# A two-block F32 network on one core: state-space preparation moved into the first feed-forward block, gate rows through DRAM, another SBUF layout

## The chip, the cores and the metric

The kernel runs on one core of a Trainium2 chip. The metric is the time of one execution on the device, in microseconds. In the profile, PE is TensorE's matmul stream, PEld its weight loads, DVE is VectorE, ACT ScalarE, POOL GpSimd, and SP is SyncE, which here only issues transfers.

## The reference

Two blocks run one after the other on 512 tokens of width 1024, both of depth 2. The first block is an attention block, which the change touches through the SBUF layout alone. The second has, in each layer, a feed-forward block, a token mixer and a second feed-forward block, each ahead of a gated residual sum:

```python
for l in range(DEPTH):
    mod = (silu(c) @ mod_w[l] + mod_b[l]).reshape(bsz, N_SUB, 3, D_MODEL)
    def pre(x, i):          return rms_norm(x, norm_pre[l, i]) * (1 + mod[:, i, 1]) + mod[:, i, 0]
    def post_add(x, y, i, w): return x + w * mod[:, i, 2] * rms_norm(y, norm_post[l, i])
    x = post_add(x, swiglu(pre(x, 0), ffn_w_in[l, 0], ffn_w_out[l, 0]), 0, 0.5)
    x = post_add(x, token_mixer(pre(x, 1), ...), 1, 1.0)
    x = post_add(x, swiglu(pre(x, 2), ffn_w_in[l, 1], ffn_w_out[l, 1]), 2, 0.5)

def s5_ssm(u, a_re, a_im, log_dt, b_re, b_im, c_re, c_im, d_skip):   # inside the mixer
    lam_bar = exp(lam * dt)                     # weights alone
    b_bar = ((lam_bar - 1) / lam)[..., None] * b  # weights alone
    states = scan(lam_bar, einsum(u, b_bar))    # over the 512 tokens
    return real(einsum(c, states)) + d_skip * u
```

The state-space part has 32 groups of 16 channels with 64 complex states each. All that depends on `a`, `log_dt`, `b` and `c` alone can be worked out before `u` is known.

## The kernel before

**Products.** All large products are F32 products made of three passes with F32R operands: each operand is held as a high and a low part, and `mm3` issues high×high, high×low and low×high (L336 to L338). The weights come through `unit`: SP loads 512 KB into a `raw` tile (3 slots, L316), ACT casts the high part into `wh` (3 slots, L319) and DVE subtracts to get the low part `wl` (3 slots, L320). Activations, and everything of 4 KB per partition, live in a pool called `big` with 34 slots. In `mm3` the weights are the stationary operand and 512 tokens move; in `tokens` (L413 to L415) the activations are stationary and the weights move, of which some are in `wh` and `wl` and the others, kept, in `big` tiles.

**Where tiles lie.** The pools get their SBUF addresses in the order in which the first tile of each tag is asked for. The built program has the tags `raw`, `wh`, `wl`, `tmp`, `hf` and `ms` at addresses that leave 32 on division by 64 bytes, since a tile `hpi` of 4 bytes is allocated ahead of them; `big` and `ones` leave 0.

**The feed-forward block** (`ffn`) goes in three parts p of 8, 7 and 7 column blocks. Each part first makes its `mid` tiles in a `glu` loop, two products (48 matmuls) per block, and then, in `tokens`, four passes over the 128-token groups that add `mid @ w_out` into `y`. POOL takes the low part of every second block (L428), DVE the others. While these run, `mod_job` streams the modulation weights of a layer through `ms` tiles and reduces them on DVE (L1001); for both layers this is over by the end of layer 0. Between p = 0 and p = 1, `gate_row` spreads a row of `mod` over the partitions by 8 F32 matmuls against the identity (L461) and two ACT copies, and `ssm_params` computes the small per-state numbers on DVE.

**The mixer** interleaves three generators by counters (`MIX`): attention, the gate products, and `ssm`. For each quarter q of 128 channels, `ssm` loads `ssmbc` (256 KB), forms the complex product `bl` with 6 DVE operations (`cplx`, L1221 to L1226), transposes it on PE (8 F32 transposes, L1246) into `gt`, forms `cl` and the rotations `cs` with 11 POOL operations on 128x512 (L1216, L1258, L1261 and `cplx`), forms the direct kernel `kt` on PE (L1276, L1279) and DVE; all of that depends on weights alone. Then come the parts that need the tokens: input products (L1290), the scan, the state `hh` on POOL and DVE (L1310 to L1315) and the output `y_ps`: per 128 columns j, j+1 direct products of 128x128 (L1322, F32) and 8 products with 32 output rows (L1325). The program's order on each engine is fixed when it is built.

Of the kernel before, what the change touches and what calls it, by code (L numbers as in the profile page):

```python
# [240 lines left out]
class Net:  # L241
    def __init__(self, ctx, tc, io, stop=None):
        self.tc, self.nc, self.io, self.stop = tc, tc.nc, io, stop
        nc = self.nc
        self.sb = ctx.enter_context(tc.tile_pool(name="sb", bufs=1))
        self.ps = ctx.enter_context(tc.tile_pool(name="ps", bufs=1, space=PSUM))
        self.dr = ctx.enter_context(tc.tile_pool(name="dr", bufs=1, space=DRAM))
        self.n, self.odd, self.turn, self.jobs, self.pace = 0, False, 0, [], None
        self.xd = io["x"]
        self.xf = [self.big() for _ in range(4)]  # L250
        self.ones = self.sb.tile([128, 128], F32, name="ones")
        nc.vector.memset(self.ones, 1.0)
        self.mhalf = self.sb.tile([128, 16], F32, name="mhalf")
        nc.vector.memset(self.mhalf, -0.5)
        self.hpi = self.sb.tile([128, 1], F32, name="hpi")
        nc.vector.memset(self.hpi, math.pi / 2)

    def constants(self):
        nc, io = self.nc, self.io
        cst = self.sb.tile([128, C_TAB], F32, name="cst")  # L260
        nc.sync.dma_start(cst, io["consts"][:, :C_TAB])
        self.cst = cst
        self.ident = cst[:, C_ID:C_ID + 128]
        self.mask = self.sb.tile([128, 3, 128], F32R, name="mask")
        for i, o in enumerate((C_ID, C_TRI, C_PERM)):
            nc.scalar.copy(self.mask[:, i], cst[:, o:o + 128])
        self.par = []
        for l in range(DEPTH):
            t = self.sb.tile([128, P_N], F32, name=f"par{l}")
            nc.sync.dma_start(t, io["params"][l])  # L270
            self.par.append(t)
# [704 lines left out]
    def mod_job(self, l):  # L976
# [29 lines left out]
        for i in range(3):  # L1006
            sc = mod[:, i * 24 + 8:i * 24 + 16]
            gt = mod[:, i * 24 + 16:i * 24 + 24]
            nc.vector.scalar_tensor_tensor(sc, in0=sc, scalar=1.0, in1=par[:, P_NPRE + 8 * i:P_NPRE + 8 * i + 8],
                                           op0=ALU.add, op1=ALU.mult)  # L1010
            nc.vector.tensor_scalar(sc, sc, 32.0, None, op0=ALU.mult)
            nc.vector.scalar_tensor_tensor(gt, in0=gt, scalar=32.0 if i == 1 else 16.0,
                                           in1=par[:, P_NPOST + 8 * i:P_NPOST + 8 * i + 8],
                                           op0=ALU.mult, op1=ALU.mult)


    def gate_row(self, l, i):

        o = self.big((128, D))
        k = i * 24 + 16  # L1020
        for m, a in enumerate(self.halves(o)):
            self.nc.scalar.copy(a, self.bcast(self.mod[l][:, k + 4 * m:k + 4 * m + 4]))
        return o
# [16 lines left out]
    def ffn(self, l, i, h, nxt, between):  # L1040
        nc = self.nc
        h = self.acts(h)
        y = [self.big((128, D)) for _ in range(4)]
        for p, n in enumerate(SPLIT_K):
            mid = self.pairs(n)
# [15 lines left out]
            for j, f in enumerate(fs):  # L1061
                if j < nh:
                    continue
                f(*[self.mblock(self.wk(f"in{i}"), h) for _ in range(2)], FULL)
                self.pace = mid[j][:, 0, 0:1].bitcast(F32)
                self.pump(2)
            acts = [(t[:, 0], t[:, 1]) for t in mid]
# [9 lines left out]
            if p == 0:  # L1077
                gate = self.gate_row(l, i)
                if i == 0:
                    self.ssm_p = self.ssm_params(l)  # L1080

        if callable(nxt):
            nxt = nxt()
# [118 lines left out]

    def ssm(self, l, P, u, ud, out):

        nc = self.nc
        v, g = nc.vector, nc.gpsimd
        d4 = [128, 4, 4, 32]

        def v4(t):
# [8 lines left out]
        def cplx(e, o, a, b, c, d, view):  # L1218
# [7 lines left out]
            e.tensor_tensor(o[:, 1], o[:, 1], t[:, 1], op=ALU.add)  # L1226

        for q in range(4):
            pq = slice(q * 4, q * 4 + 4)
# [5 lines left out]
                      for c in range(2))  # L1235
            f0, f1 = (f[:, pq].unsqueeze(3).to_broadcast(d4) for f in P["f"])
            cplx(v, bl, b0, b1, f0, f1, v4)
            bb = self.tmp(256)
            nc.scalar.copy(bb.rearrange("p (c a b) -> p c a b", c=2, a=4),
                           bl.rearrange("p c (a j b) -> p c a j b", a=4, j=4)[:, :, :, 3])  # L1240
            gt = self.big()
            for c in range(2):
                ps = self.t("aux", [128, 512])
                for i in range(4):
                    s = slice(i * 128, (i + 1) * 128)
                    nc.tensor.transpose(ps[:, s], bl[:, c, s], self.ident)  # L1246
                if c:
                    nc.scalar.copy(gt[:, c], ps)
                else:
                    v.tensor_copy(gt[:, c], ps)  # L1250
            nc.scalar.mul(bc[:, 3], bc[:, 3], -1.0)
# [14 lines left out]
            cplx(g, cs, *ta, *tb, lambda t: t.rearrange("p (a b c) -> p a b c", a=4, b=8))  # L1266
            ct, st = cs[:, 0], cs[:, 1]
            ru = self.big()
            rho = v3(ru[:, 0])
            nc.scalar.copy(rho, P["rho"][:, pq].unsqueeze(2).to_broadcast([128, 4, 128]))  # L1270
            g.memset(rho[:, :, 0:1], 0.0)
            nc.sync.dma_start(ru[:, 1], ud[q])
            yield 1
            ps = self.t("aux", [128, 512])
            for c in range(2):
                nc.tensor.matmul(ps[:, 0:128], lhsT=bb[:, c * 128:(c + 1) * 128], rhs=bc[:, 2 + c],  # L1276
                                 start=c == 0, stop=c == 1)
            for c in range(2):
# [4 lines left out]
            v.scalar_tensor_tensor(kt[:, 0], in0=self.ident, scalar=self.par[l][:, P_SD + q:P_SD + q + 1],  # L1283
                                   in1=kt[:, 0], op0=ALU.mult, op1=ALU.add)
            sp = []
            for c in range(2):
# [13 lines left out]
            g.tensor_tensor(zi, zi, t[:, 1], op=ALU.subtract)  # L1300
            v.tensor_tensor_scan(zr, ru[:, 0], zr, 0.0, op0=ALU.mult, op1=ALU.add)
            v.tensor_tensor_scan(zi, ru[:, 0], zi, 0.0, op0=ALU.mult, op1=ALU.add)
            yield 1
# [13 lines left out]
            y_ps = self.t("yps", [128, 512])  # L1317
            uq = u[q // 2][:, q % 2]
            for j in range(4):
                o = y_ps[:, j * 128:(j + 1) * 128]  # L1320
                for a in range(j + 1):
                    nc.tensor.matmul(o, lhsT=kt[:, j - a], rhs=uq[:, a * 128:(a + 1) * 128], start=a == 0, stop=False)  # L1322
                for c in range(2):
                    for i in range(4):
                        nc.tensor.matmul(o[i * 32:(i + 1) * 32], lhsT=cl[:, c, j * 128 + i * 32:j * 128 + i * 32 + 32],  # L1325
                                         rhs=hh[:, c, i * 128:(i + 1) * 128], start=False, stop=c == 1)
            t = self.big()
# [9 lines left out]
    def mixer(self, l, h, nxt, between):  # L1337
        nc, par = self.nc, self.par[l]
        P = self.ssm_p
        h = self.acts(h)  # L1340
# [44 lines left out]
        side.s = side.g = 0  # L1385
        S_ = self.ssm(l, P, u, ud, gl)
        G_ = gated()
        next(S_)
        n = 0
# [115 lines left out]
    def run(self):  # L1505
        nc = self.nc
        self.mod = [None] * DEPTH
        h1 = self.newh()

# [50 lines left out]
```

## Time and profile before

| | |
|---|---|
| time, median of 3 runs | 3297.89 us (3291.76 to 3299.95) |
| the profiled execution: time, span | 3300.94 us, 3299.2 us |
| mean granted TensorE clock | 0.991 |
| SP's transfers | 377.31 MB, 33.9% of the 16 engines' time |

The span runs from the first to the last instruction. The ends of matmuls are modelled, so a duration of a matmul in the profile is longer than the step to the next one; steps are read from starts. All transfers of the kernel before are issued by SP.

### The profile page before, as it was taken

The page shows a single profiled execution, that of the slowest core. Times are in us where ns is not written, and L with a number is a line of the kernel's source. Part 1 is how long each engine was busy: PE and PEld are TensorE (multiplying, and loading weights), DVE is VectorE, ACT ScalarE, POOL GpSimd, SP SyncE. Part 2 cuts the span into 40 slices and gives each one's busy share as a digit, 9 for nine tenths or more (in the row PEclk, how much of TensorE's full clock was granted, in tenths as well). Part 3 has the DMA queues.
Part 4 walks back from the last instruction along what each step waited for, and adds up shares of the span by engine and source line. Part 5 has one row for each costly group of instructions (what it writes and reads, how often), then busy time and mean ns, then how long its engine had stood idle before and what let it go on. Part 6 is the DMA issues. An engine that isn't in the chain of part 4 may idle for free. (4 is left out here: it accounts for less than half of the span.)

```text
span 3299.2 us, 42053 instructions
## 1 busy us (share of the span) xinstructions
PE 3192.0 (97%) x16144; PEld 2586.8 (78%) x16144; DVE 1962.5 (59%) x3525; ACT 1216.4 (37%) x2088; POOL 517.4 (16%) x560
## 2 busy tenths in 40 slices
PE   8999999999999999998999999999999989999999
PEld 8777887778788888776778888888888766788887
DVE  5797756887755847567565534634345676653334
ACT  3445323454333314433443223423234334432312
POOL 1200132000220101353001000100003351010000
PEclk9999999999999999999999999999999999999999
DMA  4243532234535636221233523322233211323323
GB/s 164 78 150 104 184 128 78 97 115 143 180 104 199 210 119 226 86 82 39 71 115 111 190 96 108 135 96 78 95 134 103 74 55 52 129 88 97 116 68 109
DMA packets 132409, 379.99 MB, mean 115 GB/s; under 512 B 14832, under 2 KB 21488, under 8 KB 132208
## 3 DMA queue, kind: packets, MB, share of 16 engines
q1 hardware_dynamic: 132208, 377.31, 33.9%
q8 instruction: 127, 2.08, 0.3%
q14 instruction: 74, 0.61, 0.1%
HBM read 358.37 MB, written 18.87 MB: 114 GB/s over the span
## 5 line engine op out<-in xcount | busy, mean ns | idle before, releaser
L336 PE MATMUL acc<-big,wh 128*128 128x512 f32 (+1 forms) x2760 | 1076.6, 390 | 6.1 <-DVE tmp L721 2.9
L337 PE MATMUL acc<-big,wh 128*128 128x512 f32 (+1 forms) x2760 | 1071.6, 388 | 0.8 <-POOL big L513 0.8
L338 PE MATMUL acc<-big,wl 128*128 128x512 f32 (+1 forms) x2760 | 1069.2, 387 | 0.9 <-DVE wl L320 0.9
L320 DVE TENSOR_TENSOR wl<-raw,wh 128x1024 fp32r<-128x1024 f32 x396 | 499.6, 1264 | 528.3 <-ACT wh L319 512.1
L319 ACT CAST wh<-raw 128x1024 fp32r<-128x1024 f32 x396 | 414.2, 1046 | 983.3 <-issue 463.0
L336 PEld LDWEIGHTS acc<-big,wh 128*128 128x128 f32 x2760 | 519.8, 188 | 122.0 <-PE acc L338 5.3
L338 PEld LDWEIGHTS acc<-big,wl 128*128 128x128 f32 x2760 | 520.3, 189 | 112.7 <-issue 1.9
L337 PEld LDWEIGHTS acc<-big,wh 128*128 128x128 f32 x2760 | 520.4, 189 | 108.0 <-issue 1.5
L1001 DVE SCALAR_TENSOR_TENSOR ms<-ms,big 128x512 f32<-128x512 f32 x288 | 199.3, 716 | 50.4 <-DMA ms<-in_modw_dram 49.9
L428 POOL TENSOR_TENSOR big<-tmp,big 128x512 fp32r<-128x512 f32 (+1 forms) x44 | 69.4, 1577 | 866.2 <-ACT big L425 866.2
L1053 DVE SCALAR_TENSOR_TENSOR tmp<-tmp,acc 128x512 f32<-128x512 f32 (+1 forms) x88 | 57.2, 650 | 152.3 <-PE acc L338 152.0
L425 ACT ACTIVATE big<-tmp 128x512 fp32r<-128x512 f32 (+1 forms) x148 | 88.0, 595 | 145.3 <-POOL tmp L877 57.0
L320 DVE TENSOR_TENSOR big<-raw,big 128x1024 fp32r<-128x1024 f32 x92 | 115.1, 1261 | 16.6 <-ACT big L319 16.2
L413 PE MATMUL acc<-big,big 128*128 128x512 f32 x288 | 113.4, 394 | 0.0
L414 PE MATMUL acc<-big,big 128*128 128x512 f32 x288 | 113.2, 393 | 0.0
L319 ACT CAST big<-raw 128x1024 fp32r<-128x1024 f32 x92 | 94.9, 1045 | 48.5 <-DMA raw<-in_w_dram 48.5
L413 PE MATMUL att<-big,big 128*128 128x512 f32 x288 | 112.8, 392 | 0.0
L414 PE MATMUL att<-big,big 128*128 128x512 f32 x288 | 112.7, 391 | 0.0
L415 PE MATMUL att<-big,big 128*128 128x512 f32 x288 | 112.5, 391 | 0.0
L415 PE MATMUL acc<-big,big 128*128 128x512 f32 x288 | 112.4, 390 | 0.0
L601 ACT ACTIVATE big<-att,sm 128x512 f32<-128x512 f32 (+2 forms) x112 | 69.6, 624 | 111.8 <-DVE sm L599 111.7
L478 ACT ACTIVATE hf<-big 128x512 f32<-128x512 f32 x80 | 50.3, 629 | 136.8 <-DVE big L1088 81.4
(387 smaller groups left out, 5152.4 us busy)
## 6 DMA issues: line engine op xcount, KB each, us to landing
raw<-in_w_dram SPq DMA_DIRECT2D x486, 512.0 KB, 3.4
ms<-in_modw_dram SPq DMA_DIRECT2D x288, 256.0 KB, 3.8
xb2l0s<-big SPq DMA_DIRECT2D x12, 512.0 KB, 2.7
big<-xb2l0s SPq DMA_DIRECT2D x12, 512.0 KB, 7.5
xb1l<-big SPq DMA_DIRECT2D x8, 512.0 KB, 2.6
big<-xb1l SPq DMA_DIRECT2D x8, 512.0 KB, 6.7
xb2l1s<-big SPq DMA_DIRECT2D x8, 512.0 KB, 2.7
big<-xb2l1s SPq DMA_DIRECT2D x8, 512.0 KB, 7.7
```

The costliest lines, as they stand in the source:

```text
L319: nc.scalar.copy(hi[:, :n], raw[:, :n])
L320: nc.vector.tensor_tensor(lo[:, :n], raw[:, :n], hi[:, :n].bitcast(F32), op=ALU.subtract)
L336: nc.tensor.matmul(ps, lhsT=hi, rhs=a, start=first, stop=False)
L337: nc.tensor.matmul(ps, lhsT=hi, rhs=b, start=False, stop=False)
L338: nc.tensor.matmul(ps, lhsT=lo, rhs=a, start=False, stop=last)
L413: nc.tensor.matmul(ps[m], lhsT=a, rhs=hi, start=c == o[0], stop=False)
L414: nc.tensor.matmul(ps[m], lhsT=a, rhs=lo, start=False, stop=False)
L415: nc.tensor.matmul(ps[m], lhsT=b, rhs=hi, start=False, stop=c == o[-1])
L425: nc.scalar.activation(hi, src, AF.Copy, scale=scale)
L428: eng.tensor_tensor(lo, src, hi.bitcast(F32), op=ALU.subtract)
L601: nc.scalar.activation(ps[j], s_ps[j], AF.Exp, bias=ng[:, j:j + 1], scale=scale, accum_out=rs[:, j:j + 1])
L1001: nc.vector.scalar_tensor_tensor(w, in0=w, scalar=0.5, in1=self.sc[m], op0=ALU.mult, op1=ALU.mult, accum_out=sums[:, n, m:m + 1])
```

## The change

Four things, independent of one another:

1. **Layout.** `hpi` is widened from 4 to 64 bytes, and the first tiles of `raw`, `wh`, `wl`, `tmp`, `hf` and `ms` are claimed at once, by a POOL memset of one column each. In the built program all six tags then leave 0 on division by 64.
2. **Gate rows.** `mod_job` stores its three gate rows to DRAM, and `gate_row` is one 512 KB load that repeats the row on all partitions. The 8 matmuls and 2 ACT copies go.
3. **Preparation.** The weight-only half of `ssm` becomes a generator `ssm_prep` that `ffn` advances by one step after each `glu` block of p = 1 and 2. Per quarter it has three steps: the elementwise work; nothing; the transposes, `gt` and `kt`. Its results (2 MB per quarter) go to DRAM by five transfers that POOL issues; the mixer's `ssm` loads them back with four 512 KB transfers on SP per quarter.
4. **Direct products.** The ten 128x128 products per quarter become four of 512, 384, 256 and 128 columns, ahead of all 32-row products.

```diff
-        self.hpi = self.sb.tile([128, 1], F32, name="hpi")
+        self.hpi = self.sb.tile([128, 16], F32, name="hpi")[:, 0:1]
         nc.vector.memset(self.hpi, math.pi / 2)
+        for tag, n, dtype in (("raw", 1024, F32), ("wh", 1024, F32R), ("wl", 1024, F32R), ("tmp", 512, F32),
+                              ("hf", 512, F32), ("ms", 512, F32)):
+            nc.gpsimd.memset(self.t(tag, [128, n], dtype)[:, 0:1].bitcast(F32), 0.0)
...
+            row = self.gates[l][i].rearrange("(k p) -> p k", p=128)
+            nc.sync.dma_start(row, gt)
...
     def gate_row(self, l, i):
         o = self.big((128, D))
-        k = i * 24 + 16
-        for m, a in enumerate(self.halves(o)):
-            self.nc.scalar.copy(a, self.bcast(self.mod[l][:, k + 4 * m:k + 4 * m + 4]))
+        self.nc.sync.dma_start(o, self.gates[l][i:i + 1].to_broadcast([128, D]))
         return o
...
                 self.pace = mid[j][:, 0, 0:1].bitcast(F32)
+                next(prep, None)
                 self.pump(2)
...
                 if i == 0:
-                    self.ssm_p = self.ssm_params(l)
+                    prep = self.ssm_prep(l, self.ssm_params(l))
+        for _ in prep:
+            pass
...
+        def store(i, t):
+            g.dma_start(ssd[q, i], t.rearrange("p a b -> p (a b)"))
...
+            store(1, cl)
+            store(2, cs)
             yield 1
+            yield 1
+            gt = self.big()
+            ...            (the transposes and copies, as before)
...
+            store(0, gt)
+            g.dma_start(ssd[q, 3, :, 0:512], bk[:, 1])
+            g.dma_start(ssd[q, 3, :, 512:1024], ru[:, 0])
+            yield 1
...
+        def load(q):
+            ts = [self.big() for _ in range(4)]
+            for i, t in enumerate(ts):
+                nc.sync.dma_start(t.rearrange("p a b -> p (a b)"), self.ssd[l][q, i])
+            uu = self.big()
+            nc.sync.dma_start(uu[:, 1], ud[q])
+            return *ts, uu
...
+            for a in range(4):
+                n = (4 - a) * 128
+                nc.tensor.matmul(y_ps[:, a * 128:], lhsT=kt[:, a], rhs=uq[:, :n], start=a == 0, stop=False)
             for j in range(4):
                 o = y_ps[:, j * 128:(j + 1) * 128]
-                for a in range(j + 1):
-                    nc.tensor.matmul(o, lhsT=kt[:, j - a], rhs=uq[:, a * 128:(a + 1) * 128], start=a == 0, stop=False)
```

PE, before, in the mixer of layer 0 at its first quarter: `aux` is the PSUM tile of the transposes, the products of 8 rows are the forget gate's.

```order
L338 MATMUL acc_12177<-big_8564,wl_12124 128x256
L1246 MATMUL aux_12256<-cst,big_12245 128x128 x4
L336 MATMUL acc_12295<-big_8558,wh_12291 8x512
L337 MATMUL acc_12295<-big_8559,wh_12291 8x512
L338 MATMUL acc_12295<-big_8558,wl_12292 8x512
...
L1246 MATMUL aux_12262<-cst,big_12245 128x128 x4
```

PE, of the change, in the first feed-forward block of layer 0, after the sixth product of p = 1: L1282 is the old L1246, L1289 and L1292 are the old L1276 and L1279, L340 to L342 the old L336 to L338.

```order
L342 MATMUL acc_10164<-big_4282,wl_10161 128x512
L1282 MATMUL aux_10197<-cst,big_10003 128x128 x4
L1282 MATMUL aux_10203<-cst,big_10003 128x128 x4
L340 MATMUL acc_10247<-big_4276,wh_10243 128x512
L341 MATMUL acc_10247<-big_4277,wh_10243 128x512
L342 MATMUL acc_10247<-big_4276,wl_10244 128x512
L1289 MATMUL aux_10209<-big_10001,big_10011 128x128 x2
L1292 MATMUL aux_10209<-big_10014,big_10011 128x384 x2
```

The transposes and the products of `kt` left the mixer; the other three quarters stand after the twelfth product of p = 1 and after the fourth and tenth of p = 2, and layer 1 has the same.

PE, before, the direct and the 32-row products of the first quarter (`yps` is their PSUM tile):

```order
L338 MATMUL acc_12494<-big_8564,wl_12491 128x512
L1322 MATMUL yps_12520<-big_11726,big_12243 128x128
L1325 MATMUL yps_12520<-big_12480,big_12269 32x128 x8
L1322 MATMUL yps_12520<-big_11726,big_12243 128x128 x2
L1325 MATMUL yps_12520<-big_12480,big_12269 32x128 x8
```

PE, of the change, the same place:

```order
L1364 MATMUL yps_12708<-big_11957,big_12477 128x512
L1364 MATMUL yps_12708<-big_11957,big_12477 128x384
L340 MATMUL acc_12682<-big_8575,wh_12678 128x512
...
L1364 MATMUL yps_12708<-big_11957,big_12477 128x256
L1364 MATMUL yps_12708<-big_11957,big_12477 128x128
L1369 MATMUL yps_12708<-big_12668,big_12475 32x128 x32
```

The direct products stand ahead of all 32-row products now, and one 24-matmul product stands between them.

POOL, before, in p = 1 of the same feed-forward block (L396 claims a `mid` tile, L428 is the low part of every second block, L997 claims an `ms` tile):

```order
L396 CAST big_9917<-ones 128x1
L428 TENSOR_TENSOR big_9912<-tmp_10069,big_9912 128x512
L997 COPY ms_10165<-big_9913 128x1
...
L428 TENSOR_TENSOR big_9914<-tmp_10241,big_9914 128x512
```

POOL, of the change, the same place (`ssd` is the DRAM tensor of the results; L432 is the old L428):

```order
L1272 MEMSET big_10011 128x4
L1300 DMA ssd_10000<-big_10011 128x512
L1225 TENSOR_TENSOR big_10014<-big_10001,big_9785 128x512
...
L1238 DMA ssd_10000<-big_10014 128x1024
L1235 TENSOR_TENSOR big_10022<-big_10022,big_10023 128x512
L432 TENSOR_TENSOR big_9918<-tmp_10109,big_9918 128x512
L1238 DMA ssd_10000<-big_10022 128x1024
...
L1238 DMA ssd_10000<-big_10196 128x1024
```

Between two low parts of `mid` POOL now has 11 operations of 128x512 and five transfers to issue, of which the one of `gt` waits for PE's transposes and their copies.

## Rows read from the trace of the kernel before

**Rows 1.** The page, busy time of each engine: us, share of the span, instructions.

```profile
PE 3192.0 (97%) x16144; PEld 2586.8 (78%) x16144; DVE 1962.5 (59%) x3525; ACT 1216.4 (37%) x2088; POOL 517.4 (16%) x560
```

**Rows 2.** Group by form, L1246 on PE: count, busy us, mean ns, idle before, releasers.

```profile
L1246 PE MATMUL aux<-cst,big 128*128 128x128 f32 x64 | 11.7, 312 | 27.6 <-DVE big L1223 12.6 <-DVE big L1226 11.4 <-ACT big L924 3.6
```

**Rows 3.** Windows of layer 0's mixer, then two short ones: length, busy time, granted clock.

```profile
1307.00:1687.00 380.00, 351.60 (x2053) 279.00 (x2052) 250.34 (x343) 151.53 (x271) 109.74 (x99) 0.98 0.23 75
...
1357.00:1367.00 10.00, 6.88 (x27) 0.83 0.35 109
...
2707.00:2717.00 10.00, 8.50 (x44) 0.84 0.23 80
```

**Rows 4.** Timeline of PE, products with `wh` and `wl` stationary: start, duration.

```profile
1072.04 0.40 PE L336 MATMUL acc<-big,wh 128*128 128x512 f32 x1
...
1074.86 0.39 PE L336 MATMUL acc<-big,wh 128*128 128x512 f32 x1
```

**Rows 5.** Timeline of PE in `tokens`, moving operand first in `big`, then in `wh`, `wl`.

```profile
1026.24 0.39 PE L414 MATMUL acc<-big,big 128*128 128x512 f32 x1
...
1029.86 0.39 PE L415 MATMUL att<-big,big 128*128 128x512 f32 x1
...
1032.90 0.39 PE L413 MATMUL att<-wh,big 128*128 128x512 f32 x1
```

**Rows 6.** Timeline of PE, products of 256 columns: stationary in `wh`, then in `big`.

```profile
30.02 0.28 PE L338 MATMUL acc<-big,wl 128*128 128x256 f32 x1
...
30.73 0.28 PE L338 MATMUL acc<-big,wl 128*128 128x256 f32 x1
...
31.33 0.28 PE L336 MATMUL att<-big,big 128*128 128x256 f32 x1
...
32.29 0.28 PE L338 MATMUL att<-big,big 128*128 128x256 f32 x1
```

**Rows 7.** Groups by form: count, busy us, mean ns, idle before.

```profile
L336 PE MATMUL acc<-big,wh 128*128 128x512 f32 x2472 | 992.3, 402 | 6.1 <-DVE tmp L721 2.9 <-DVE tmp L870 2.7 <-DVE s L1111 0.3
...
L413 PE MATMUL acc<-wh,big 128*128 128x512 f32 x192 | 76.8, 400 | 0.8 <-ACT big L425 0.8
L336 PE MATMUL acc<-big,wh 128*128 128x256 f32 x272 | 76.4, 281 | 0.0
```

**Rows 8.** Timeline of PE at a gate row: L461 up to the next product.

```profile
1067.45 1.95 PE L461 MATMUL aux<-cst,mod 128*128 128x128 f32 x16
1069.15 0.48 PE L336 MATMUL acc<-big,wh 128*128 128x512 f32 x1
```

**Rows 9.** Timeline of PE: a quarter's output products, and the `kt` product.

```profile
1368.61 1.46 PE L1279 MATMUL aux<-big,tmp 128*128 128x384 f32 x4
...
1394.17 0.38 PE L1322 MATMUL yps<-big,big 128*128 128x128 f32 x2
1396.92 0.43 PE L1325 MATMUL yps<-big,big 128*32 128x128 f32 x8 [2.37 <-DVE big L1314]
...
1401.62 0.65 PE L1325 MATMUL yps<-big,big 128*32 128x128 f32 x16
1402.20 0.50 PE L336 MATMUL acc<-big,wh 128*128 128x512 f32 x1
```

**Rows 10.** Timelines of DVE and of POOL in the mixer, the first preparation.

```profile
1351.60 0.69 DVE L1221 TENSOR_TENSOR big<-big,pw 128x512 f32<-128x512 f32 x1 [5.83 <-DMA big<-in_ssmbc_dram]
1352.21 1.57 DVE L1222 TENSOR_TENSOR big<-big,pw 128x512 f32<-128x512 f32 x1
...
1351.71 4.50 POOL L1216 TENSOR_TENSOR big<-big,big 128x512 f32<-128x512 f32 x3 [26.64 <-DMA big<-in_ssmbc_dram]
```

**Rows 11.** Windows of DVE, p = 1 and 2 of the first feed-forward blocks.

```profile
1069.00:1307.00 238.00, 163.85 (x430) 1.00 0.54 184
2249.00:2487.00 238.00, 110.25 (x242) 1.00 0.30 104
```

**Rows 12.** The page, transfers: KB each, median us from issue to landing.

```profile
raw<-in_w_dram SPq DMA_DIRECT2D x486, 512.0 KB, 3.4
```

More of the change, by code (lines that the diff above doesn't have):

```diff
@@ L254, in __init__ @@
         nc.vector.memset(self.mhalf, -0.5)
-        self.hpi = self.sb.tile([128, 1], F32, name="hpi")
+        self.hpi = self.sb.tile([128, 16], F32, name="hpi")[:, 0:1]
         nc.vector.memset(self.hpi, math.pi / 2)
+        for tag, n, dtype in (("raw", 1024, F32), ("wh", 1024, F32R), ("wl", 1024, F32R), ("tmp", 512, F32),
+                              ("hf", 512, F32), ("ms", 512, F32)):
+            nc.gpsimd.memset(self.t(tag, [128, n], dtype)[:, 0:1].bitcast(F32), 0.0)
+        self.mask = self.sb.tile([128, 3, 128], F32R, name="mask")
     def constants(self):
@@ L263, in constants @@
         self.ident = cst[:, C_ID:C_ID + 128]
-        self.mask = self.sb.tile([128, 3, 128], F32R, name="mask")
         for i, o in enumerate((C_ID, C_TRI, C_PERM)):
@@ L1043, in ffn @@
         y = [self.big((128, D)) for _ in range(4)]
+        prep = iter(())
         for p, n in enumerate(SPLIT_K):
@@ L1201, in ssm_params, with ssm_prep @@
         return dict(rho=r[:, 3], tc=tc_, ts=ts_, l=(lr, li), f=(fr, fi))
-    def ssm(self, l, P, u, ud, out):
+    def ssm_prep(self, l, P):
         nc = self.nc
@@ L1207, in ssm @@
         d4 = [128, 4, 4, 32]
+        self.ssd[l] = ssd = self.dr.tile([4, 4, 128, 1024], F32, name=f"ssd{l}")
         def v4(t):
@@ L1237, in ssm @@
             cplx(v, bl, b0, b1, f0, f1, v4)
-            bb = self.tmp(256)
+            ru = self.big()
+            bb = ru[:, 1, 0:256]
             nc.scalar.copy(bb.rearrange("p (c a b) -> p c a b", c=2, a=4),
                            bl.rearrange("p c (a j b) -> p c a j b", a=4, j=4)[:, :, :, 3])
[L1241 to L1250, printed above, removed]
             nc.scalar.mul(bc[:, 3], bc[:, 3], -1.0)
@@ L1266, in ssm @@
             cplx(g, cs, *ta, *tb, lambda t: t.rearrange("p (a b c) -> p a b c", a=4, b=8))
-            ct, st = cs[:, 0], cs[:, 1]
-            ru = self.big()
             rho = v3(ru[:, 0])
@@ L1271, in ssm @@
             g.memset(rho[:, :, 0:1], 0.0)
-            nc.sync.dma_start(ru[:, 1], ud[q])
+            store(1, cl)
+            store(2, cs)
             yield 1
+            yield 1
+            gt = self.big()
+            for c in range(2):
+                ps = self.t("aux", [128, 512])
+                for i in range(4):
+                    s = slice(i * 128, (i + 1) * 128)
+                    nc.tensor.transpose(ps[:, s], bl[:, c, s], self.ident)
+                if c:
+                    nc.scalar.copy(gt[:, c], ps)
+                else:
+                    v.tensor_copy(gt[:, c], ps)
             ps = self.t("aux", [128, 512])
@@ L1284, in ssm, with v3, mul @@
                                    in1=kt[:, 0], op0=ALU.mult, op1=ALU.add)
+            store(0, gt)
+            g.dma_start(ssd[q, 3, :, 0:512], bk[:, 1])
+            g.dma_start(ssd[q, 3, :, 512:1024], ru[:, 0])
+            yield 1
+    def ssm(self, l, u, ud, out):
+        nc = self.nc
+        v, g = nc.vector, nc.gpsimd
+        def v3(t):
+            return t.rearrange("p (a b) -> p a b", a=4)
+        def mul(o, a, b):
+            g.tensor_tensor(o, a, b, op=ALU.mult)
+        def load(q):
[5 more added lines that the diff above has]
+            return *ts, uu
+        for q in range(4):
+            gt, cl, cs, kr, ru = load(q)
+            ct, st = cs[:, 0], cs[:, 1]
+            kt = v3(kr[:, 0])
+            yield 1
             sp = []
@@ L1300, in ssm @@
             g.tensor_tensor(zi, zi, t[:, 1], op=ALU.subtract)
-            v.tensor_tensor_scan(zr, ru[:, 0], zr, 0.0, op0=ALU.mult, op1=ALU.add)
-            v.tensor_tensor_scan(zi, ru[:, 0], zi, 0.0, op0=ALU.mult, op1=ALU.add)
+            v.tensor_tensor_scan(zr, kr[:, 1], zr, 0.0, op0=ALU.mult, op1=ALU.add)
+            v.tensor_tensor_scan(zi, kr[:, 1], zi, 0.0, op0=ALU.mult, op1=ALU.add)
             yield 1
@@ L1325, in ssm @@
                         nc.tensor.matmul(o[i * 32:(i + 1) * 32], lhsT=cl[:, c, j * 128 + i * 32:j * 128 + i * 32 + 32],
-                                         rhs=hh[:, c, i * 128:(i + 1) * 128], start=False, stop=c == 1)
+                                         rhs=hh[:, c, i * 128:(i + 1) * 128], start=False, stop=j == 3 and c == 1)
             t = self.big()
@@ L1338, in mixer @@
         nc, par = self.nc, self.par[l]
-        P = self.ssm_p
         h = self.acts(h)
@@ L1385, in mixer @@
         side.s = side.g = 0
-        S_ = self.ssm(l, P, u, ud, gl)
+        S_ = self.ssm(l, u, ud, gl)
         G_ = gated()
@@ L1507, in run @@
         self.mod = [None] * DEPTH
+        self.ssd = [None] * DEPTH
+        self.gates = [self.dr.tile([3, D], F32, name=f"gates{l}") for l in range(DEPTH)]
         h1 = self.newh()
```

## The prediction

> **What bounds the kernel now.** I read the page first: PE is busy for 3192.0 of 3299.2 us [rows 1], so about 107 us of the span are gaps on PE, and everything else must come out of what PE itself does. Then PE's gaps by line: the largest by far stands ahead of the eight F32 transposes per quarter of the mixer, L1246, with 27.6 us over 64 matmuls, nearly all of it waiting for the DVE operations of `cplx` [rows 2]. The windows show what that does beside the gap itself: over the mixer of layer 0 the granted clock is 0.98, and in the ten-us windows in which the transposes wait it is 0.83 to 0.84 [rows 3]; there are six stretches of this kind in both layers, with 80 us of windows. [...]
>
> Then the step of PE where it is fed without gaps, read from starts, since ends are modelled. With `wh` and `wl` stationary twelve steps take 1074.86 - 1072.04 = 2.82 us, 0.235 us each [rows 4]. In `tokens`, with both operands in `big`, 16 steps take 1029.86 - 1026.24 = 3.62 us, 0.226 each, and as soon as the moving operand comes out of `wh` and `wl` the 13 steps from 1029.86 to 1032.90 take 0.234 each [rows 5]. Same engine, same number of columns, same clock; what differs is the tile, and by the addresses in the program `wh` and `wl` sit 32 bytes off the multiple of 64 on which `big` sits.
>
> **The change part by part.** All against the profiled execution, 3300.9 us, which is 3 us above the median of the runs.
>
> *Layout.* L336, L337 and L338 have 2472 matmuls of 512 columns each with `wh` or `wl` stationary, 7416 [rows 7]; `tokens` has 192 per line and PSUM tile with these moving, six such groups, 1152 [rows 7]. If the addresses are the cause, each step falls by 7.5 ns [rows 5] to 8.7 [rows 4, 5]; the ends are rounded to 10 ns and the stretches are short, so I count 7: 7416 x 7 = 52 us and 1152 x 7 = 8 us. Against it stand the products of 256 columns: with `wh` stationary six steps take 30.73 - 30.02 = 0.71 us, 118 ns; with `big` stationary eight take 0.96, 120 ns [rows 6]. There the aligned tile is 2 ns slower. With 272 per line and PSUM tile (I take both tiles alike), 1632 x 2 = 3 us come back. Bounds 0 (the tile's address is not the cause) and -71 (8.7 ns throughout). I take -57, since the change of step within one pass of `tokens` is the nearest row.
>
> *Preparation, what goes.* The 27.6 us of waits at L1246 go if their place in `ffn` is late enough: DVE's product of quarter q is queued two steps (four 24-matmul products, some 22 us) ahead of the transposes. The matmuls themselves are moved and cost the same. The lower clock after these gaps goes too: over the six stretches (1 - clock) x length is 1.6 to 1.8 us for each ten-us window with a gap, 10 us in all, and part of it lies in the gaps; I take -8. Together -36; lower bound -20, if each transposes' gap is only made half as long.
>
> *Preparation, what comes.* Per quarter DVE gets 6 operations of 0.69 us, two copies or products of the same size and a small one, about 6 us, and POOL 11 operations. The rows of the mixer show that the two hinder each other: L1221 takes 0.69 us and L1222, same shape, 1.57 while POOL works, and three POOL operations take 4.50 [rows 10]. So each POOL operation costs DVE up to 0.9 us. Four quarters: 24 us of work and up to 4 x 11 x 0.9 = 40 of blocking. In layer 0, p = 1 and 2 have 238 us with DVE busy for 163.9 [rows 11]; the layout shortens the stretch by 7 us. That leaves 67 us idle for 64 us: DVE is full. In layer 1, without the modulation weights, 110.3 are busy [rows 11] and nothing is short. When DVE is late, `wl` is late next, and with it PE at L342, then the `raw` slot and SP's queue. Where the modulation's operations can slip nothing is lost, and where two loads of work meet PE waits: I take +14 for layer 0 (bounds 0 and 40, the full blocking) and +2 for layer 1 (0 to 10).
>
> [...]
>
> *Preparation, in the mixer.* SP gets four loads of 512 KB per quarter, in front of the next `raw` loads in its queue. One lands in 3.4 us [rows 12]; four in a row cost 14 at most, while three `raw` slots ahead cover 3 x 24 x 0.234 = 17 us of PE. So they fit, unless one waits for a `big` slot: bounds 0 and +20, I take +6. The 11 POOL and 6 DVE operations leave the mixer, where DVE has 250 of 380 us [rows 3]; this shortens waits of attention too, which I don't count.
>
> *Gate rows.* From L461's start to the next product is 1069.15 - 1067.45 = 1.70 us of PE [rows 8], six times: -10 us. The load is issued early and used in the residual sum; the store of 1024 elements one by one is done long before. Cost 0, hidden behind a whole part p of `ffn`; if it came late, DVE's sum would wait a few us, six times.
>
> *Direct products.* A quarter's output products run from 1394.17 to 1402.20, 8.03 us, of which 2.54 are waiting for DVE. The 32-row ones take four times about 0.6 us (0.58 from 1401.62 to 1402.20), 2.5; the direct ones 3.0 [rows 9]. The new ones stream 1280 columns, two records each: at the rate of the 384-column records of `kt`, four in at most 1.46 us [rows 9] of which the last one's modelled end is no step, about 0.33 each, that is 6.7 x 0.33 = 2.2 us. -0.8 per quarter, -6 for eight; bounds 0 and -12 (the wait covered by them as well).
>
> Sum: -57 - 36 - 10 - 6 + 14 + 2 + 6 = -87, 3214 us profiled, and less 3, **3211 us**.
>
> **The rivals.**
>
> *The address is not what makes the step longer.* `wh` and `wl` also differ from `big` in that they have just been written by ACT and DVE, and rows 6 show an aligned tile that is no faster. Then the 57 us stay: 3268 us. For the addresses speaks that the step changes within one pass, at the very tile. [...]
>
> *DVE in layer 0 is over its limit.* Blocking in full and colliding with the modulation: +40 to +60 in place of +14, at about 3250 with the layout's gain. Against it: the modulation's operations can slip.
>
> [...]
>
> **How the numbers follow.** A measurement of this kernel tells about 0.3%, 10 us, from no change. My forecast, 3211 (3185 to 3240): 0.55. The layout without gain, about 3268 (3250 to 3285): 0.24, of which a small part comes within 10 us. DVE over its limit, about 3250: 0.09. Slower by POOL's queue, 3310 to 3340: 0.06. More gain than I count, from attention's waits in the mixer, 3165 to 3185: 0.06. To leave out no more than 2 in 10, the range goes from 3178 to 3285. Faster by over 0.3% 0.88, within it 0.05, slower 0.07.
>
> **What the profile of the changed kernel would show.** The step of L340 to L342 at 0.226 us in a `glu` loop, and no change of step within a pass of `tokens`, for the layout; at 0.234 still, the first rival. No wait at L1282, and the clock in the mixers near 1.00. [...] PE without L461 between p = 0 and 1. Waits of L1333 for the loads of `ssd` should not exceed a few us. What would make the prediction wrong most easily is the layout, by 57 us.

## The result, and the profile after

The changed kernel takes 3322.52 us (median of 4, 3321.58 to 3325.22); the kernel before takes 3296.58 us (median of 4). The ratio is 1.0081, 95% interval 1.0064 to 1.0099: slower by 26 us. The prediction was 3211 us with a range up to 3285; it had 0.07 on slower. The profiled execution has a span of 3321.1 us and a mean granted clock of 0.983, where it was 0.991.

First, the page of the changed kernel, busy time by engine:

```profile
PE 3172.6 (96%) x15952; PEld 2576.4 (78%) x15952; DVE 2012.3 (61%) x3525; ACT 1207.1 (36%) x2076; POOL 508.5 (15%) x606
```

PE is busy for 19 us less than before [rows 1] and idle for 41 us more. Its waits by releaser (total us, times, longest):

```profile
PE acc L417 <- ACT big L323: 17.9, 2, 9.0
PE acc L340 <- DVE tmp L1057: 17.8, 3, 7.7
PE att L579 <- ACT big L605: 13.0, 17, 2.5
PE acc L340 <- DVE tmp L874: 12.7, 1, 12.7
PE acc L340 <- ACT wh L323: 11.9, 3, 4.1
PE aux L1289 <- DVE big L1286: 10.6, 2, 8.3
```

No line of the transposes (L1282) is left, as intended. New are waits for a free `acc` (L1057 is the `glu` operation that reads it), for kept weights (L417), for `wh`, for the PSUM tile of `kt` (L1289), and one of 12.7 us at L874, in the first block. By stage, windows with the columns of [rows 3], the first feed-forward block's p = 1 and 2 of layer 0, its mixer, and the same of layer 1:

```profile
1075.00:1378.80 303.80, 263.04 (x1090) 207.07 (x1089) 237.37 (x470) 79.92 (x124) 87.70 (x102) 0.92 0.51 176
1378.80:1719.70 340.90, 327.03 (x1930) 262.56 (x1929) 200.20 (x303) 145.22 (x255) 39.20 (x47) 0.99 0.32 110
2275.20:2556.50 281.30, 255.40 (x1090) 203.31 (x1089) 185.46 (x278) 79.47 (x124) 83.86 (x92) 0.96 0.35 123
2556.50:2897.30 340.80, 326.87 (x1930) 262.52 (x1929) 200.24 (x303) 145.31 (x255) 39.30 (x47) 0.99 0.32 110
```

Before, the mixer of layer 0 took 380 us [rows 3], and that of layer 1:

```profile
2487.00:2871.00 384.00, 352.81 (x2058) 279.56 (x2057) 249.48 (x339) 151.48 (x271) 110.48 (x99) 0.97 0.23 74
```

The mixers became some 40 us shorter each, 83 in both, more than predicted. The stretches in which the work now lies were 238 to 239 us [rows 11] and became 304 and 281: 107 us back, with the clock at 0.92 and 0.96. Of these 107, 66 are idle time of PE (length less busy time, 66.7 us in the two rows above, 0.9 before) and 21 are the moved products themselves, the transposes and `kt` (summed over starts); the rest is, by estimate, in the main the lower clock. That is where the gain went, and more. What happens there shows in DVE's groups (count, busy us, mean ns):

```profile
L1233 DVE TENSOR_TENSOR big<-big,pw 128x512 f32<-128x512 f32 x8 | 81.1, 10138 | 0.0
L1231 DVE TENSOR_TENSOR big<-big,pw 128x512 f32<-128x512 f32 x8 | 29.9, 3737 | 0.0
```

An operation that took 0.69 us alone [rows 10] takes 10 us on average. POOL's transfers stand on the page in a queue of their own, `software_dynamic`, and are called software transfers below. The timelines of POOL, DVE, ACT and PE at the first quarter:

```profile
1093.76 0.76 POOL L1300 DMA_DIRECT2D ssd<-big  x1 [0.31 <-DVE pw L1208]
1094.55 3.15 POOL L1225 TENSOR_TENSOR big<-big,big 128x512 f32<-128x512 f32 x3
...
1105.46 1.04 POOL L1234 TENSOR_TENSOR big<-big 128x512 f32<-128x512 f32 x1
1106.46 0.58 POOL L1238 DMA_DIRECT2D ssd<-big  x1
...
1094.08 12.98 DVE L1231 TENSOR_TENSOR big<-big,pw 128x512 f32<-128x512 f32 x1
1106.98 1.91 DVE L1233 TENSOR_TENSOR big<-big,pw 128x512 f32<-128x512 f32 x1
...
1110.13 0.40 ACT L1252 COPY big<-big 128x256 f32<-128x256 f32 x1 [16.34 <-DVE big L1235]
...
1110.74 0.80 PE L340 MATMUL acc<-big,wh 128*128 128x512 f32 x1 [7.72 <-DVE tmp L1057]
```

One DVE operation stands still while POOL runs eleven operations at 1.04 to 1.29 us each, where the first three took 1.5 in [rows 10], and it ends right after POOL turns to issuing a transfer. (A quarter has twelve of them; the prediction counted 11.) In the rows of before the two took turns; here they don't. All eight quarters have one such DVE operation of 12.8 to 13.0 us. Behind it stand `glu` on DVE, the cast of `wh` on ACT (it follows L1252 in ACT's program, which waited 16.34 us for DVE), and with these PE; afterwards PE's records last 0.80 and 0.63 us, with a granted clock of 0.50 from 1110.7 to 1116.0 us.

The wait at L874 is another matter. The timelines of SP, ACT and PE in the second layer of the first block:

```profile
841.72 1.63 SPq L1020 DMA_DIRECT2D gates<-mod  x3
843.91 20.60 SPq L320 DMA_DIRECT2D raw<-in_w_dram  x3
...
861.85 1.04 ACT L323 CAST big<-raw 128x1024 fp32r<-128x1024 f32 x1 [12.71 <-DMA raw<-in_w_dram]
...
865.40 0.80 PE L340 MATMUL acc<-big,wh 128*128 128x512 f32 x1 [12.71 <-DVE tmp L874]
```

Three stores of gate rows, 1024 elements of 4 bytes each, go out just ahead of a weight tile, issued at 843.91, for whose data ACT waits until 861.85, 18 us. On the page, among the transfers (KB, us to landing), the gate stores stand as

```profile
gates<-mod SPq DMA_DIRECT2D x6, 4.0 KB, 14.1
```

4 KB in 14.1 us, beside 512 KB of weights in 3.7. And the step of the products with `wh` is 232 ns (median over the pairs of starts in the trace), 2 ns less than before, where 7 were counted.

### The profile page after: what moved, and what is told of

Same layout as the page of the kernel before. It is cut to its first block, busy times and chain, and to the rows that moved or that the text cites. A ratio compares the mean times of both kernels' runs of the same rounds, so it can differ in the third digit from the quotient of the medians.

```text
span 3321.1 us, 41885 instructions
## 1 busy us (share of the span) xinstructions
PE 3172.6 (96%) x15952; PEld 2576.4 (78%) x15952; DVE 2012.3 (61%) x3525; ACT 1207.1 (36%) x2076; POOL 508.5 (15%) x606
## 5 line engine op out<-in xcount | busy, mean ns | idle before, releaser
L340 PE MATMUL acc<-big,wh 128*128 128x512 f32 (+1 forms) x2760 | 1080.5, 392 | 45.5 <-DVE tmp L1057 17.8
L342 PE MATMUL acc<-big,wl 128*128 128x512 f32 (+1 forms) x2760 | 1068.7, 387 | 2.0 <-DVE wl L324 1.9
L324 DVE TENSOR_TENSOR wl<-raw,wh 128x1024 fp32r<-128x1024 f32 x396 | 488.4, 1236 | 549.2 <-ACT wh L323 520.4
L340 PEld LDWEIGHTS acc<-big,wh 128*128 128x128 f32 x2760 | 523.1, 190 | 161.5 <-DVE tmp L1057 19.4
L342 PEld LDWEIGHTS acc<-big,wl 128*128 128x128 f32 x2760 | 522.0, 189 | 114.4 <-DVE wl L324 6.1
L432 POOL TENSOR_TENSOR big<-tmp,big 128x512 fp32r<-128x512 f32 (+1 forms) x44 | 70.4, 1600 | 744.2 <-ACT big L429 744.2
L417 PE MATMUL acc<-big,big 128*128 128x512 f32 x288 | 114.5, 398 | 17.9 <-ACT big L323 17.9
L417 PE MATMUL att<-big,big 128*128 128x512 f32 x288 | 113.5, 394 | 0.0
```

The costliest lines, as they stand in the source:

```text
L324: nc.vector.tensor_tensor(lo[:, :n], raw[:, :n], hi[:, :n].bitcast(F32), op=ALU.subtract)
L340: nc.tensor.matmul(ps, lhsT=hi, rhs=a, start=first, stop=False)
L342: nc.tensor.matmul(ps, lhsT=lo, rhs=a, start=False, stop=last)
L417: nc.tensor.matmul(ps[m], lhsT=a, rhs=hi, start=c == o[0], stop=False)
L432: eng.tensor_tensor(lo, src, hi.bitcast(F32), op=ALU.subtract)
```

## The experiments

Each ratio is to the kernel before in the same runs, with its 95% interval. "The changed kernel" means all four parts.

**Layout alone** (e1): the hunk of the diff at `hpi` and `mask`, on the kernel before.

> The kernel before with the layout part alone. By the prediction's layout step the time falls by 57 us, to about 3240 us, with steps of 0.226 us in the glu loops. By the trace of the changed kernel, where the median step of the products with wh and wl went from 234 to 232 ns only, it falls by about 7416 x 1.6 ns = 12 us, to about 3285 us, and tokens still changes its step where the moving operand comes out of wh and wl.

Measured: 3290.26 us, ratio 0.9973 (0.9964 to 0.9982), 9 us (7 by the medians). The timeline of PE in the `glu` loop, the place of [rows 4], 12 steps:

```profile
1071.52 0.39 PE L339 MATMUL acc<-big,wh 128*128 128x512 f32 x1
...
1074.31 0.39 PE L339 MATMUL acc<-big,wh 128*128 128x512 f32 x1
```

2.79 us for 12, 0.2325 each. The tiles lie on multiples of 64 bytes now and the step has hardly moved: alignment to 64 isn't the cause.

**Stores issued by SP** (e2), on the changed kernel:

```diff
-            g.dma_start(ssd[q, i], ...)
+            nc.sync.dma_start(ssd[q, i], ...)      (and so the stores of kt and rho)
```

> The changed kernel with the stores of the preparation issued by SP in place of POOL. Theory A: a DVE operation that meets POOL while POOL issues a software transfer is left waiting through the whole chain of POOL operations behind it (12.9 us in each of the 8 quarters). Without transfers on POOL the two engines alternate as in the kernel before: no DVE operation over 2.4 us apart from scans and reciprocals, and some 60 to 80 us of the loss in the first feed-forward blocks go, to about 3250 us. Theory B: the chain of POOL operations starves DVE whatever stands ahead of it: DVE operations of 12 to 14 us remain, and the time stays at 3305 to 3335 us.

Measured: 3295.25 us, ratio 0.9992 (0.9983 to 1.0001), 27 us less than the changed kernel. No DVE operation but the reciprocals takes over 2.4 us; POOL at the first chain:

```profile
1099.50 4.62 POOL L1225 TENSOR_TENSOR big<-big,big 128x512 f32<-128x512 f32 x3
1104.08 1.74 POOL L1261 TENSOR_TENSOR big<-big,big 128x512 f32<-128x512 f32 x1
```

1.54 us each: the two engines take turns again, with the same operations. Theory A holds for the lockout, those 12.8 to 13.0 us, but the kernel gains 27 us, not 60 to 80. The engines still hinder each other (1.54 us, where these POOL operations took 1.05 in the changed kernel), and SP's weight loads now stand behind stores that wait for POOL, 31.3 us in all; how much each of these costs wasn't tried. So 27 us is not what the lockout costs: e12 below ends it with the stores left on POOL, and gains 48.

**Gate rows by matmul** (e3), on the changed kernel: `gate_row` and `mod_job` as in the kernel before.

> The changed kernel with the gate rows made by matmuls again. The stores of 4-byte elements go, and with them the wait of 12.7 us for a raw load in the second layer of the first block and the lower clock behind it; 10 us of matmuls come back. If the part is worth what the prediction counted, the kernel becomes 10 us slower (3332 us); if its stores cost what the trace suggests, it stays within 5 us (3315 to 3325 us).

Measured: 3323.31 us, ratio 1.0076 (1.0062 to 1.0090), against 1.0081 with the gate rows by transfer. The part is worth nothing by the medians: what the matmuls gave, the stores took (the wait at L874 falls from 12.7 us to 2.8 in two pieces). The profiled execution, at 3317.68 us the fastest of the four, holds one more thing. Seven of its eight chains lock DVE out. The other, the first of layer 1, begins directly behind a transfer as well, and the engines take turns from its first operation on:

```profile
2291.58 0.61 POOL L1300 DMA_DIRECT2D ssd<-big  x1 [0.30 <-DVE pw L1205]
2292.21 4.20 POOL L1225 TENSOR_TENSOR big<-big,big 128x512 f32<-128x512 f32 x3
...
2291.73 0.69 DVE L1230 TENSOR_TENSOR big<-big,pw 128x512 f32<-128x512 f32 x1
2292.33 1.06 DVE L1208 TENSOR_TENSOR pw<-s,s 128x16 f32<-128x16 f32 x1
```

Here a DVE operation, begun during the transfer, was still running when the chain began, and it was not held. What sets this chain apart isn't shown.

**The preparation's POOL operations on DVE** (e4), on the changed kernel:

```diff
-            g.tensor_tensor(o, a, b, op=ALU.mult)
+            v.tensor_tensor(o, a, b, op=ALU.mult)
...
-            cplx(g, cs, *ta, *tb, ...)
+            cplx(v, cs, *ta, *tb, ...)             (and so the two sums of cl)
```

> The changed kernel with the 11 POOL operations of each quarter's preparation on DVE; POOL only issues the stores. If DVE's being locked out during POOL's chain is what costs 107 us in the first feed-forward blocks, no DVE operation of over 2.4 us is left there, the 11 operations cost DVE 7.6 us per quarter, and the time falls to 3235 to 3265 us. If it is the amount of DVE work, or the wait of ACT for the product, the time stays above 3300 us.

Measured: 3257.45 us, ratio 0.9880 (0.9867 to 0.9892), 65 us less than the changed kernel. The operations take on DVE what they take alone:

```profile
L1225 DVE TENSOR_TENSOR big<-big,big 128x512 f32<-128x512 f32 x32 | 20.6, 683 | 0.0
```

DVE runs 96 operations more than in the changed kernel and the kernel is faster, so the amount of DVE work was not what cost 107 us. The wait at L874 stays, 14.1 us.

**Only rho and kt stored by SP** (e5), on the changed kernel; the stores of `cl`, `cs` and `gt` stay on POOL.

> The changed kernel with two of a quarter's five stores (rho and kt, which stand directly ahead of the next chain on POOL) issued by SP; the stores of cl, cs and gt stay on POOL. If a DVE operation is locked out because it meets a software transfer directly ahead of the chain, most of the operations of 12.9 us go or become shorter and the time falls towards that of all stores on SP (3295 us). If any software transfer in the queue is enough, the eight operations of 12.9 us stay, and 3322 us.

Measured: 3315.20 us, ratio 1.0038 (1.0024 to 1.0051). Neither all nor none: four of the eight lockouts are left. The kernel holds both cases. POOL and DVE at a chain without lockout:

```profile
1128.43 0.53 POOL L1238 DMA_DIRECT2D ssd<-big  x1
1129.84 0.11 POOL L1272 MEMSET big<- 128x4 f32 x1 [0.88 <-ACT big L1271]
1129.90 3.66 POOL L1225 TENSOR_TENSOR big<-big,big 128x512 f32<-128x512 f32 x3
...
1130.84 0.69 DVE L1231 TENSOR_TENSOR big<-big,pw 128x512 f32<-128x512 f32 x1
```

and at one with:

```profile
1264.35 0.57 POOL L1238 DMA_DIRECT2D ssd<-big  x1
1264.91 0.12 POOL L1272 MEMSET big<- 128x4 f32 x1
1264.98 3.17 POOL L1225 TENSOR_TENSOR big<-big,big 128x512 f32<-128x512 f32 x3
...
1265.47 12.06 DVE L1231 TENSOR_TENSOR big<-big,pw 128x512 f32<-128x512 f32 x1
```

The same DVE operation arrives within the first POOL operations in both. In the first POOL had waited 0.88 us between its transfer and the chain, in the second the chain follows at once. The other three lockouts of this kernel have a transfer directly ahead too. Of the other three chains without lockout, one stands 1.4 us behind its transfer, and the first of each layer has none ahead. The MEMSET of 128x4 between transfer and chain, in both timelines, doesn't prevent the lockout; the DVE operation that is held arrives after it.

**Direct products alone** (e6): the last hunk of the diff, on the kernel before.

> The kernel before with the long direct products alone. The prediction counted -6 us (0 to -12), 3291 us. The mixers of the changed kernel became 83 us shorter, some 40 more than the prediction's terms for them; if the direct products are the cause of the rest, this kernel is 30 us or more faster (3267 us or less).

Measured: 3279.32 us, ratio 0.9930 (0.9918 to 0.9942), 21 us: between the two. The mixer of layer 0, columns as in [rows 3]:

```profile
1307.00:1678.00 371.00, 349.01 (x2004) 276.35 (x2003) 249.35 (x344) 152.10 (x272) 109.48 (x99) 0.97 0.24 79
```

Some 9 us shorter, 11 in layer 1. Summed over starts, and without waits, the direct products' steps fell from 24.4 to 18.2 us, as the prediction counted, and those of the 32-row products, whose number is the same, from 22.7 to 17.7, which the prediction put at nothing. In the steps of before, the first direct product behind a 32-row one takes 0.24 us on average and the last ahead of one 0.22, where 0.12 is the mean between two direct products; a 32-row group ends with a step of 0.2 us, and there are fewer groups now. Beside these 11 us PE waits less: its idle time in the whole span falls from 107 to 93 us, 4 of it for the state `hh` ahead of the 32-row products and 7 in attention (L575, L576). The granted clock of the mixer didn't rise (0.97, 0.98 before).

**Weights at the lowest addresses** (e7): the layout part, with the six claims ahead of `big`.

> The layout part alone with raw, wh, wl, tmp, hf and ms at the lowest addresses and big above them (before: big below). If the region of SBUF in which a tile lies sets the step, L336 to L338 in the glu loops fall from 232 to about 227 ns and the time by some 35 us against the layout alone, to about 3255 us. If what matters is something else about wh and wl (they are written all the while), the step stays at 231 to 234 ns and the time at 3285 to 3295 us.

Measured: 3257.35 us, ratio 0.9865 (0.9852 to 0.9878), 43 us. The median step of L336 to L338's successors is 227 ns, and that of `tokens` with moving `wh` and `wl` too. It looked like the region; but `big`, now up to 219264 and so where `wh` had been, also has 227.

**Weights behind `big`, same residue** (e9), and **`big` shifted** (e10). In the layout of the change `big` leaves 128 on division by 2048 and `wh` 768; in e7 both leave 128. e9 keeps `wh` high and makes it 128; e10 keeps it low and makes `big` 768.

```diff
+        (e9: the six claims here, behind self.xf and ahead of self.ones)
...
+        (e10: the six claims first, then ones, mhalf and hpi, 640 bytes, then big)
```

> The layout part alone, but with the six tags claimed directly behind big (wh at 168064, high in SBUF as in the kernel before, and at 128 on division by 2048, as big is); in the layout of the change wh leaves 768. With raw, wh and wl at the lowest addresses the step was 227 ns and the kernel took 3257 us; there both left 128 too. If the residue decides, the step is 227 ns here too and the time about 3257 us. If the region decides, the step is 232 ns and the time about 3290 us.

> The low layout with 640 bytes between ms and big: wh leaves 128 on division by 2048, big 768. If what decides is that the two operands of a product have the same residue, the step of L336 to L338 goes back to about 232 ns and the time to about 3290 us, and products with both operands in big stay at 227. If the residue of wh alone decides, 227 ns and 3257 us. If big's own residue were to decide, products with both in big become slower too.

Measured: e9 3261.45 us, ratio 0.9893 (0.9878 to 0.9907); e10 3290.72 us, ratio 0.9980 (0.9971 to 0.9990). The timelines of PE, e9 first (10 steps), then e10 (12):

```profile
1071.66 0.39 PE L339 MATMUL acc<-big,wh 128*128 128x512 f32 x1
...
1073.93 0.39 PE L340 MATMUL acc<-big,wh 128*128 128x512 f32 x1
```

```profile
1071.62 0.39 PE L339 MATMUL acc<-big,wh 128*128 128x512 f32 x1
...
1074.41 0.39 PE L339 MATMUL acc<-big,wh 128*128 128x512 f32 x1
```

0.227 and 0.2325 us. Products with both operands in `big` stay at 227 in both kernels. So in these kernels it is neither the region nor one tile's own address, but whether the tiles of the two operands leave the same residue.

**Three POOL memsets in the chain** (e12), on the changed kernel. They write a half tile that is overwritten afterwards and read nothing.

```diff
             t = self.big()
+            for _ in range(3):
+                g.memset(t[:, 0], 0.0)
             mul(v4(cl[:, 0]), cv[0], lv[0])
```

> The changed kernel with three more POOL memsets of 128x512 (which read nothing) per quarter, which stand between the first POOL operations of the chain behind the software transfer. If DVE is held for as long as POOL's reading operations follow each other behind a transfer, the first memset lets it in: no DVE operation over 4 us in the first part, and the time falls by 30 us or more. If DVE is held until the next transfer or the end of the chain, operations of 13 to 15 us stay, and 3315 to 3340 us.

Measured: 3274.73 us, ratio 0.9931 (0.9914 to 0.9948): three operations more per quarter, and 48 us less than the changed kernel. POOL and DVE at the first quarter:

```profile
1095.63 0.76 POOL L1302 DMA_DIRECT2D ssd<-big  x1 [0.30 <-POOL big L1274]
1096.40 0.55 POOL L1260 MEMSET big<- 128x512 f32 x1
1096.89 1.09 POOL L1225 TENSOR_TENSOR big<-big,big 128x512 f32<-128x512 f32 x1
1097.90 0.54 POOL L1260 MEMSET big<- 128x512 f32 x1
...
1096.56 1.97 DVE L1233 TENSOR_TENSOR big<-big,pw 128x512 f32<-128x512 f32 x1
1098.46 1.57 DVE L1232 TENSOR_TENSOR big<-big,big 128x512 f32<-128x512 f32 x1
```

The chain, with a memset ahead, begins directly behind a transfer. The DVE operation of 1096.56 waits while L1225 runs in 1.09 us, and gets its turn at the next memset: it ends 0.63 us after that memset's start. No DVE operation of this kernel but the reciprocals takes more than 3.2 us.

**Both causes mended** (e8, e11). e8 has the preparation on DVE, stores the gate rows as 8 rows of 512 bytes, and makes `kt` a step after the transposes; e11 adds the claims of e7.

```diff
-            row = self.gates[l][i].rearrange("(k p) -> p k", p=128)
-            nc.sync.dma_start(row, gt)
+        ps = self.t("aux", [128, 512])
+        nc.tensor.transpose(ps[0:72, 0:128], mod, self.ident)
+        o = self.tmp()
+        nc.vector.tensor_copy(o[0:72, 0:128], ps[0:72, 0:128])
+        for i in range(3):
+            nc.sync.dma_start(self.gates[l][i].rearrange("(k p) -> k p", p=128), o[i * 24 + 16:i * 24 + 24, 0:128])
```

> The changed kernel with the preparation's elementwise work on DVE, the gate rows transposed on PE first so that each is stored as 8 rows of 512 bytes, and the kt products one step after the transposes. With the work on DVE alone the kernel takes 3257 us; the stores of 4-byte elements cost it a wait of 14 us in the first block, and kt's wait for the PSUM tile that DVE frees some 6 us. If these are what they seem, it falls to 3235 to 3245 us; if the wait for raw has another cause, it stays within 5 us of 3257.

> The version with the preparation on DVE and gate rows stored as rows of 512 bytes (3233.5 us), with raw, wh, wl, tmp, hf and ms at the lowest addresses. The low layout was worth 33 us over the layout of the change (3290 to 3257). If the two add up, 3195 to 3208 us; if a faster PE runs into DVE's limit in the first feed-forward blocks, 3208 to 3225 us.

Measured: e8 3233.51 us, ratio 0.9797 (0.9783 to 0.9810); e11 3210.97 us, ratio 0.9736 (0.9722 to 0.9751), faster than both kernels. The wait of 14.1 us at L874 is gone in e8, and of the low layout's 33 us e11 keeps 23. How the 24 us between e4 and e8 divide between the row stores and the later `kt` wasn't tried. In its profile DVE has 195 of 240 us busy in p = 1 and 2 of layer 0, columns as in [rows 3]:

```profile
1060.00:1300.00 240.00, 232.40 (x1021) 189.04 (x1020) 194.58 (x489) 69.93 (x99) 31.57 (x49) 0.99 0.63 221
```

## Why the prediction was wrong

The kernel took 111 us more than the 3211 us of the prediction. By the parts as measured, the layout makes up 48 of them (9 in place of 57) and the preparation some 70 (a loss of some 56 in place of a gain of 14); the gate rows add 10, and the direct products take 15 away. So two steps failed, the cause behind the layout's term and the price of the preparation where it lands.

*Layout, -57 us: the cause was wrong.* That the step changes at the tile was read rightly from [rows 5]; that it is the 32 bytes was a guess from addresses, and e1 gives 9 us for it. e7, e9 and e10 show the cause: 232 to 234 ns when `wh` and `big` differ in their residue, 227 when they agree. The gain was there, 43 us in e7, but the change doesn't make it. The first rival had this outcome for the kernel (the 57 us stay), though not this reason. The shortest steps of 512 columns measured here are 226 to 227 ns ([rows 5], e7, e9).

*Preparation, what goes, -36 us: right.* No wait at L1282. What the gaps did to the clock the trace of before shows: behind the 3.12 us gap of the first quarter it was 0.51 from 1361.9 to 1365.4 us, and 1.00 from there to 1368.0. The mixers lost 83 us, and nearly all of them are accounted for: 21 by the direct products (e6), the 36 counted for the waits and the clock of [rows 2, 3], and 22 that are the moved products themselves (in the kernel before, summed over starts, 7.7 us of transposes, L1246, and 14.1 of `kt`, L1276 and L1279). Those come back in the feed-forward blocks, as the prediction had it with "cost the same". Attention waits hardly less than before, 22 us (L579, L580) against 24 (L575, L576), though DVE's work in a mixer fell from 250 to 200 us and POOL's from 110 to 39.

*Preparation, what comes, +16 us: the step that failed.* It reads "each POOL operation costs DVE up to 0.9 us", taken from [rows 10], where the two alternate. In the changed kernel one DVE operation loses a whole chain, 12 us, and with it the order of `glu`, casts and PSUM tiles: 65 us in layer 0 and 42 in layer 1, of which 21 are the moved products. The lockout alone costs some 48 us (e12). Layer 1, which had DVE to spare, shows that it isn't the sum of DVE's work, as the prediction had it; so does e4. e2, e5 and e12 show what it hangs on: every lockout stands where the chain follows directly on a software transfer, none where POOL was idle for 0.9 us in between or had no transfer, and with memsets in the chain a DVE operation got its turn 1.3 us after it had begun, at the second of them (e12). The condition isn't the whole one: of the 20 such chains in the changed kernel, e3 and e5, 19 lock DVE out and one doesn't (e3). I predicted what is late next as `wl` at L342; it was the `acc` tile, the cast `wh`, the `kt` tile and the kept weights. By what mechanism a transfer takes DVE's turn away isn't shown by these runs.

*Slower by POOL's queue* (3310 to 3340 us, 0.06) named the right engine. That POOL's own work comes late by its queue was the author's estimate, and no run shows it: the transfers themselves are issued in 0.5 to 0.8 us and land in 3.0 to 3.5 us (medians), and PE waits 1.5 us for L432 as it did for L428. It is not confirmed by its figure being near.

*Mixer's loads, +6 us:* no wait of L1333 for them is in the trace; 0 would have been right.

*Gate rows, -10 us: 0* (e3). The matmuls went, and the store, for which I wrote "done long before", delayed what stands behind it: SP's next weight tile, 18 us where 3.7 is the median. A transfer's cost was sought in its own result, not in the queue.

*Direct products, -6 us: 21* (e6). The direct products' own steps came out as counted (24.4 to 18.2 us); left out were the 5 us of the 32-row products' steps and the shorter waits.

The parts measured apart, -9 (layout), -21 (direct) and 0 (gates), leave +56 for the preparation. That is an estimate, which takes the parts to add up. By the windows it is some -60 in the mixers, and 107 in the blocks where it went, with the 21 us of moved products in both and a few us of the layout's and the gate rows' gain inside the second.

## What to carry to other kernels

Moving work off the bounding stage is paid for at the place where it lands: look there at what it shares (here turns with another engine, SP's queue, PSUM tiles), and bound the price by a whole chain of the other engine (12 to 13 us here), not by one of its operations (0.9). Before long POOL chains beside DVE work, keep software transfers out of POOL's queue, or put the work on DVE, where an operation took 0.68 us here in place of 1.05 to 1.3 on POOL. And when a difference follows a tile, vary region, alignment and relative offset apart: two of the three explain the same rows.

## What the runs showed of the hardware

- Directly behind a software transfer issued by POOL, a chain of POOL operations on SBUF held one DVE operation with two SBUF inputs for 12 to 13 us (19 of 20 chains in the changed kernel, e3 and e5), until POOL turned to its next transfer. In e12 a held operation got its turn at a memset within the chain and took 1.97 us. Without the transfer the engines alternate at 1.5 us ([rows 10], e2). There the turns are one instruction each; in the lockout POOL's next ten instructions went ahead of the waiting one.
- A 512-column product with `wh` or `wl` stationary steps every 227 ns when the tiles of moving and stationary operand leave the same residue on division by 2048 (e7, e9), and every 232 to 234 ns with residues 640 (the changed kernel, e1, e10) or 608 bytes apart (the kernel before). Which smaller power of two would do wasn't tried. With 256 columns the median steps of the kernel before are 117 ns with different residues and 120 with the same.
- A store of 1024 elements of 4 bytes landed after 14.1 us (median of six); the weight tile issued behind three of them came after 18 us, where 3.7 is the median.
- At a change between F32 products of 128 rows and products of 32 rows the steps were longer (0.24 and 0.22 us, where 0.12 is the mean between two direct products): with 48 changes fewer, and as many columns, their own steps fell by 11 us (e6), about half in either kind.
